# A two-layer hybrid attention trunk: o^T of a chunk loaded and split earlier, a layer's first scores held back longer

## The chip, the cores and the metric

The kernel runs on one core of a Trainium2 chip. Its engines are TensorE (PE: matmuls and transposes; PEld is the loading of its weights), VectorE (DVE), ScalarE (ACT), GpSimd (POOL) and SyncE (SP), which here only issues DMAs. Each engine works through its own queue in order and waits on semaphores for the others. The metric is the device time of one execution in microseconds (us), the median of several runs.

## The reference

Sixteen learned tokens are put ahead of a sequence of 1024, so there are 1040 positions of width 1024, in float32. Then come two layers and a last norm:

```python
for l in range(DEPTH):                       # 2 layers
    hn = rmsnorm(h, norm_gain[l])
    proj = hn @ w_in[l]
    dq, dk, dv, dg, fq, fk, fv, ff, fg = jnp.split(proj, split_points, axis=-1)
    # group 1: 4 differential heads, two softmaxes each, rotary on 16 of 64 columns
    do = diff_attention(rope(dq), rope(dk), dv, lam, chunk_ids)   # p0 - lam * p1
    do = rmsnorm(do, subln_gain[l]) * (1.0 - lam_init) * silu(dg)
    # group 2: 8 forgetting heads, causal, bias from a running sum of log-sigmoids
    fo = forgetting_attention(fq, fk, fv, cumsum(log_sigmoid(ff + b)), positions) * silu(fg)
    h = h + jnp.concatenate([do, fo], axis=-1) @ w_out[l]
out = rmsnorm(h, final_gain)[:, N_META:N_META + seq]
```

## The kernel before

Everything is kept transposed, features on the partitions and positions along the free axis. The 1040 positions are three chunks, c = 0, 1, 2, of 336, 384 and 320 columns, and nine blocks of at most 128. A float32 product is made of three passes over parts rounded to fewer bits: a tensor is split into `hi` (a rounded copy, by ACT) and `lo` (what is left, by a subtraction on DVE or POOL), and hi x hi, lo x hi and hi x lo are summed. So a projection of one chunk for 128 output features is 8 x 3 = 24 matmuls (`mtile`), and gives the processor back after every 6. The split activations of chunk c lie in the tiles `acth` and `actl`, one pair of buffers for each chunk.

A layer has eight head pairs p: 0 to 3 are the differential heads, 4 to 7 two forgetting heads each. For each pair there are projections k, q and a gate g, and four v units of two pairs each. In `q_unit` and `k_unit` a differential head's chunk is turned by `rotate`: ACT copies it out of PSUM, DVE shuffles, POOL and DVE multiply, DVE adds, and then ACT and DVE split it. `Unit` is one attention step (pair, head, chunk): scores on PE, the smallest entry found and the bias added on DVE (tile `mn`), the exponential on ACT, the turn of the probabilities on PE (`transp`, tile `tp`), their split by ACT and DVE (`ath`, `atl`), and the product with v on PE (`av`, tile `po`). Three PSUM banks hold scores. `finish` writes o^T of that step to DRAM (`oscr`).

PE's order is written out while the program is built. `attention` yields, before each step, the time at which it could run and what it needs, and `layer` fills in projections from `fills` until the clock of a small model, `pe.t`, has come that far; a ratio spreads the projections over the pairs. `when[...]` says when a result will be there: for q of a chunk it is `pe.t` plus `LROT` or `LFOX`. The other engines' orders come from a list scheduler, which may put an instruction ahead of earlier ones.

When all projections are placed, `fills` goes on to the output projection. `hc_load` brings the residual of a chunk from DRAM, `out_load` four of the eight 128-row pieces of o^T, into the chunk's `actl` tile, and `out_split` splits them; for the first four (the differential heads) it first loads a row of norm factors from `nscr`, broadcast to a tile `tc`, and multiplies. `tc` has three buffers, which gates and rotations use too. Then `out_main` makes 8 x 24 matmuls of the chunk, with weights loaded and split on the way, and `out_tail` makes the next layer's activations, or the output.

The step has three parts here. (1) Chunks 0 and 1 get their `hc_load`, `act_tiles` and first `out_load` one after the other, each followed by 4.52 us of the model's time (`OL`) before its `out_split`. (2) For each chunk, when its last pair is done, the second `out_load` and `out_split` follow. (3) The model waits `OW` = 7.53 us after the chunk's last gate or pair, and `out_main` starts. Of chunk 2, part (1) comes behind `out_main` of chunk 0.

Of the kernel before, what the change touches and what calls it, by code (L numbers as in the profile page):

```python
# [54 lines left out]
LS, LSC, LT, L1S, LROT, LFOX = ((1.9, 0.0033), (3.4, 0.0042)), 0.7, 2.4, 4.87, 8.0, 5.61  # L55
OT1, OT2, OT3, OW, OL = 2.46, 4.57, 2.54, 7.53, 4.52

LLF, LCUM, LHN = 13.0, 10.0, 8.0
CMAX, SLACK, RMIN, RMAX, STEP, FR0, FR1 = 3.17, 0.4, 0.03, 2.52, 2, 2, 2
# [27 lines left out]
def trunk_kernel(ctx, tc, x, meta, norm_gain, w_in, fbias, lq1, lk1, lq2, lk2,  # L87
# [87 lines left out]
    pe = Clock()  # L175
    const = {}
    when = {}
# [280 lines left out]
    def q_unit(l, p, acts, box):  # L458
# [5 lines left out]
        for c in range(3):  # L464
# [16 lines left out]
            box["q", p, c] = (qq, ql)  # L481
            when["q", p, c] = pe.t + (LROT if diff else LFOX)
            yield
# [101 lines left out]
    def gate(l, p, acts, box):  # L585
# [18 lines left out]
        for c in range(3):  # L604
# [21 lines left out]
            if keep:  # L626
                box["kept"] += 1
                box["gs", p, c] = g
            yield

# [405 lines left out]
    def fills(l, acts, box, new):  # L1036

        unit = {"k": k_unit, "q": q_unit, "g": gate, "v": v_unit}
        todo = ORDER.replace("|", "").split()
        other = None  # L1040
        while todo:
            u = todo.pop(0)
# [14 lines left out]
            if other is not None and (not todo or todo[0][0] == "v"):  # L1057
                yield from other
                other = None
        ts, hcs = [], []  # L1060
        for c in range(3):
            hcs.append(hc_tiles())
            hc_load(hcs[c], c)
            ts.append(act_tiles(c))
            out_load(l, c, ts[c], 0)
            t0 = pe.t
            while pe.t < t0 + OL and (7, 2) not in box["done"]:
                yield True
            out_split(l, c, ts[c], 0)
            if c == 1:  # L1070
                break
        tail = iter(())
        for c in range(3):
            while (7, c) not in box["done"]:
                yield True
            out_load(l, c, ts[c], 4)
            out_split(l, c, ts[c], 4)
            t0 = max(box["done"][7, c], box["done"].get(("g", c), 0.0))
            while pe.t < t0 + OW and (7, 2) not in box["done"]:
                yield True  # L1080
            ob = []
            yield from weave(out_main(l, c, hcs[c], ts[c], ob), tail)
            drive(tail)
            tail = out_tail(l, c, hcs[c], ob, new)
            if c == 0:
                hcs.append(hc_tiles())
                hc_load(hcs[2], 2)
                ts.append(act_tiles(2))
                out_load(l, 2, ts[2], 0)
                out_split(l, 2, ts[2], 0)  # L1090
# [122 lines left out]
```

## Time and profile before

| | us |
|---|---|
| median of 3 runs | 1607.82 |
| lowest and highest | 1603.9, 1608.37 |
| the profiled execution | 1611.42 |
| its span, first to last instruction | 1609.4 |
| PE busy | 1492.9 (93% of the span) |
| DVE busy | 1047.0 (65%) |
| ACT busy | 827.1 (51%) |
| POOL busy | 689.3 (43%) |
| mean granted TensorE clock | 0.968 |

Busy times of different engines overlap, so they don't add up to the span. A granted clock of 1.0 is the higher of TensorE's two levels, 2.4 GHz, and 0.5 the lower, 1.2 GHz. The profiled execution is 3.6 us above the median of the runs.

### The profile page before, as it was taken

Reading aid. Unit: us, or ns where it says so; the run is one execution under the profiler, and the core shown is the slowest. Engines: PE = TensorE matmul, PEld = TensorE weight load, DVE = VectorE, ACT = ScalarE, POOL = GpSimd, SP = SyncE. Lnnn points to the kernel's source line nnn. Section 1 sums busy time; section 2 is a strip of 40 time slices with the busy share of each in tenths; the row PEclk is TensorE's granted clock in tenths of the full one; section 3 lists DMA queues with packets and bytes.
Section 4 is the critical chain, followed back from the end, with each engine's and each line's share of the span. In section 5 each row is a group of like instructions: output and inputs, shape, how many; then the busy total and the mean of one; then the engine's idle time right before and its main releaser. Section 6 shows DMA issues by size and latency. Waiting matters only on the chain.

```text
span 1609.4 us, 30140 instructions
## 1 busy us (share of the span) xinstructions
PE 1492.9 (93%) x9932; PEld 1421.5 (88%) x9932; DVE 1047.0 (65%) x3026; ACT 827.1 (51%) x2067; POOL 689.3 (43%) x1125
## 2 busy tenths in 40 slices
PE   5988999899999999897898999998999999997997
PEld 4888999898999999887888899998899999996897
DVE  6488867765746565767565986685656555657564
ACT  6455555544655565543334655554455545654543
POOL 3353422313444344456755353230344442443664
PEclk9999999999999999989999999999999999997999
DMA  9242311312232323555434232130322332334554
GB/s 241 65 112 68 100 46 44 63 32 81 63 69 67 100 59 99 154 177 145 142 80 95 73 82 80 35 78 20 69 65 70 55 94 57 92 115 141 154 151 138
DMA packets 181180, 147.72 MB, mean 92 GB/s; under 512 B 19592, under 2 KB 176576, under 8 KB 181024
## 3 DMA queue, kind: packets, MB, share of 16 engines
q1 hardware_dynamic: 180416, 143.60, 33.8%
q10 hardware_dynamic: 608, 2.20, 0.4%
q8 instruction: 79, 1.29, 0.3%
q14 instruction: 77, 0.63, 0.1%
HBM read 117.36 MB, written 28.38 MB: 91 GB/s over the span
## 4 chain that ended last, share of the span: by engine, by line
PE 33%; DVE 10%; DMA 6%; issue 4%; POOL 3%; ACT 2%; SPq 0%; ACTq 0%; DVEq 0%; POOLq 0%
PE pj L181 22%; PE po L181 4%; PE sc L181 4%; PE tp L185 3%; DMA wst<-in_w_out_dram 2%; DVE wlo L265 1%; DVE e L656 1%; POOL wlo L265 1%; DMA oscr<-ta 1%; DMA wst<-in_w_in_dram 1%; DVE kt L430 1%; DMA tc<-nscr 1%; DVE actl L430 1%; DMA cb<-in_rope_dram 1%; DVE atl L748 1%
## 5 line engine op out<-in xcount | busy, mean ns | idle before, releaser
L181 PE MATMUL pj<-acth,whi 128*128 128x320 f32 (+2 forms) x1536 | 518.8, 338 | 14.7 <-DVE hc L943 9.3
L181 PE MATMUL pj<-acth,wlo 128*128 128x320 f32 (+2 forms) x1536 | 498.3, 324 | 0.4 <-DVE wlo L265 0.3
L181 PE MATMUL pj<-actl,whi 128*128 128x320 f32 (+2 forms) x1536 | 497.8, 324 | 0.0
L265 POOL TENSOR_TENSOR wlo<-wst,whi 128x256 fp32r<-128x256 f32 (+1 forms) x320 | 250.8, 792 | 242.2 <-ACT whi L261 155.3
L181 PEld LDWEIGHTS pj<-acth,whi 128*128 128x128 f32 x1536 | 296.0, 193 | 18.3 <-DVE hc L943 6.5
L181 PEld LDWEIGHTS pj<-acth,wlo 128*128 128x128 f32 x1536 | 295.6, 192 | 1.8 <-POOL wlo L265 0.7
L181 PEld LDWEIGHTS pj<-actl,whi 128*128 128x128 f32 x1536 | 294.2, 192 | 0.0
L664 ACT ACTIVATE e<-e,mn 80x80 f32<-80x80 f32 (+8 forms) x288 | 225.2, 782 | 133.9 <-DVE mn L656 131.6
L748 DVE TENSOR_TENSOR atl<-tp,ath 128x320 fp32r<-128x320 f32 (+8 forms) x432 | 190.6, 449 | 98.5 <-ACT ath L747 94.8
L747 ACT ACTIVATE ath<-tp 128x320 fp32r<-128x320 f32 (+8 forms) x432 | 166.9, 403 | 150.2 <-PE tp L185 143.1
L261 ACT ACTIVATE whi<-wst 128x256 fp32r<-128x256 f32 (+1 forms) x304 | 124.7, 414 | 133.6 <-DMA wst<-in_w_out_dram 54.1
L181 PE MATMUL sc<-kt,qq 128*128 128x296 f32 (+9 forms) x480 | 176.0, 369 | 18.2 <-DVE mn L656 11.9
L185 PE MATMUL tp<-ident,e 128*128 128x128 f32 (+2 forms) x1080 | 182.0, 276 | 6.1 <-DVE e L716 4.6
L697 POOL TENSOR_SCALAR e<-e,rl 80x80 f32<-80x80 f32 (+2 forms) x144 | 109.1, 758 | 166.8 <-DVE rl L696 165.7
L181 PE MATMUL po<-ath,v 128*128 128x256 f32 (+5 forms) x576 | 166.7, 330 | 13.2 <-ACT ath L747 13.0
L181 PE MATMUL pj<-whi,acth 128*128 128x256 f32 (+3 forms) x576 | 168.0, 292 | 5.4 <-DVE v L430 4.2
L181 PE MATMUL pj<-wlo,acth 128*128 128x256 f32 (+3 forms) x576 | 165.6, 288 | 2.0 <-POOL wlo L265 1.0
L181 PE MATMUL pj<-whi,actl 128*128 128x256 f32 (+3 forms) x576 | 165.4, 287 | 1.8 <-POOL actl L406 0.9
L181 PE MATMUL po<-atl,v 128*128 128x256 f32 (+5 forms) x432 | 138.5, 321 | 22.4 <-DVE atl L748 22.1
L181 PE MATMUL sc<-kt,ql 128*128 128x296 f32 (+9 forms) x480 | 158.1, 331 | 0.0
L185 PEld LDWEIGHTS tp<-ident,e 128*128 128x128 f32 (+2 forms) x1080 | 137.5, 140 | 12.6 <-DVE e L716 5.4
L265 DVE TENSOR_TENSOR wlo<-wst,whi 128x256 fp32r<-128x256 f32 (+1 forms) x128 | 87.7, 691 | 60.0 <-POOL whi L263 53.9
(167 smaller groups left out, 2479.9 us busy)
## 6 DMA issues: line engine op xcount, KB each, us to landing
wst<-in_w_in_dram SPq DMA_DIRECT2D x256, 128.0 KB
wst<-in_w_out_dram SPq DMA_DIRECT2D x192, 128.0 KB
cb<-in_rope_dram SPq DMA_DIRECT2D x20, 320.0 KB
cb<-cscr SPq DMA_DIRECT2D x12, 520.0 KB
cb<-in_rope_dram SPq DMA_DIRECT2D x16, 384.0 KB
oscr<-ta SPq DMA_DIRECT2D x26, 160.0 KB
cb<-in_rope_dram SPq DMA_DIRECT2D x12, 336.0 KB
oscr<-ta SPq DMA_DIRECT2D x20, 192.0 KB
```

The source lines that it names most:

```text
L181: nc.tensor.matmul(o, a, b, start=start, stop=stop)
L185: nc.tensor.transpose(o, a, idn)
L261: nc.scalar.activation(hi, sg_, AF.Copy)
L265: eng.tensor_tensor(lo, sg_, hi.bitcast(F32), ALU.subtract)
L430: nc.vector.tensor_tensor(lo, src, hi.bitcast(F32), ALU.subtract)
L656: nc.vector.tensor_tensor_reduce(e[rows, a:b], pt[rows, :b - a], bias(a, b)[rows, :], op0=ALU.add, op1=ALU.min, scale=1.0, scalar=least, a ...
L664: nc.scalar.activation(e[rows, :ext], e[rows, :ext], AF.Exp, scale=-1.0, bias=mn[rows, len(pcs) - 1:len(pcs)], accum_out=l[rows, :])
L697: nc.gpsimd.tensor_scalar(e[rows, :ext], e[rows, :ext], r[rows, 0:1], 1.0, ALU.mult, ALU.mult)
L747: nc.scalar.activation(ah[:kz, n0:w], tp[:kz, n0:w], AF.Copy)
L748: nc.vector.tensor_tensor(al[:kz, n0:w], tp[:kz, n0:w], ah[:kz, n0:w].bitcast(F32), ALU.subtract)
```

## The change

A new function `early(c)` is called by `gate`, when the last of the eight gates of a chunk is placed, for chunks 0 and 1. It does the chunk's `hc_load`, `act_tiles`, and both parts of `out_load` and `out_split`; the second part only if the chunk's last pair is done by then. The wait `OL` is gone. What could not be loaded then is loaded inside the loop over `out_main`'s steps of an earlier chunk, as soon as the last pair of that chunk is done, or at the old place. Besides, the first pair's q counts as ready 6.0 us later in the model (`LQ0`), so that PE's order holds more projections ahead of a layer's first scores.

```diff
--- before.py
+++ after.py
@@ -53,9 +53,9 @@
 
 
 LS, LSC, LT, L1S, LROT, LFOX = ((1.9, 0.0033), (3.4, 0.0042)), 0.7, 2.4, 4.87, 8.0, 5.61
-OT1, OT2, OT3, OW, OL = 2.46, 4.57, 2.54, 7.53, 4.52
-
-LLF, LCUM, LHN = 13.0, 10.0, 8.0
+OT1, OT2, OT3, OW = 2.46, 4.57, 2.54, 7.53
+
+LLF, LCUM, LHN, LQ0 = 13.0, 10.0, 8.0, 6.0
 CMAX, SLACK, RMIN, RMAX, STEP, FR0, FR1 = 3.17, 0.4, 0.03, 2.52, 2, 2, 2
 COST = {"k": 11.4, "q": 11.4, "g": 11.4, "v": 25.7, "h": 0.0}
 FADD = [0.0, 0.0, 0.0, 0.0, 0.0, 0.0, 0.0, 20.0]
@@ -479,7 +479,7 @@
                 nc.gpsimd.tensor_scalar(qq[s][ro, o:w], qq[s][r, o:w].bitcast(F32), 1.0, 1.0,
                                         ALU.mult, ALU.mult)
             box["q", p, c] = (qq, ql)
-            when["q", p, c] = pe.t + (LROT if diff else LFOX)
+            when["q", p, c] = pe.t + (LROT if diff else LFOX) + LQ0 * (p == 0)
             yield
 
 
@@ -626,6 +626,9 @@
             if keep:
                 box["kept"] += 1
                 box["gs", p, c] = g
+            box["gd"][c] += 1
+            if box["gd"][c] == 8 and c < 2:
+                box["early"](c)
             yield
 
 
@@ -1038,6 +1041,20 @@
         unit = {"k": k_unit, "q": q_unit, "g": gate, "v": v_unit}
         todo = ORDER.replace("|", "").split()
         other = None
+        ts, hcs, whole = [], [], set()
+
+        def early(c):
+
+            hcs.append(hc_tiles())
+            hc_load(hcs[c], c)
+            ts.append(act_tiles(c))
+            for k0 in (0, 4):
+                if k0 == 0 or (7, c) in box["done"]:
+                    out_load(l, c, ts[c], k0)
+                    out_split(l, c, ts[c], k0)
+                    if k0:
+                        whole.add(c)
+        box["gd"], box["early"] = [0] * 3, early
         while todo:
             u = todo.pop(0)
             now = head_norms(l, box) if u == "h" else unit[u[0]](l, int(u[1]), acts, box)
@@ -1057,29 +1074,25 @@
             if other is not None and (not todo or todo[0][0] == "v"):
                 yield from other
                 other = None
-        ts, hcs = [], []
-        for c in range(3):
-            hcs.append(hc_tiles())
-            hc_load(hcs[c], c)
-            ts.append(act_tiles(c))
-            out_load(l, c, ts[c], 0)
-            t0 = pe.t
-            while pe.t < t0 + OL and (7, 2) not in box["done"]:
-                yield True
-            out_split(l, c, ts[c], 0)
-            if c == 1:
-                break
         tail = iter(())
         for c in range(3):
             while (7, c) not in box["done"]:
                 yield True
-            out_load(l, c, ts[c], 4)
-            out_split(l, c, ts[c], 4)
+            if c not in whole:
+                whole.add(c)
+                out_load(l, c, ts[c], 4)
+                out_split(l, c, ts[c], 4)
             t0 = max(box["done"][7, c], box["done"].get(("g", c), 0.0))
             while pe.t < t0 + OW and (7, 2) not in box["done"]:
                 yield True
             ob = []
-            yield from weave(out_main(l, c, hcs[c], ts[c], ob), tail)
+            for _ in weave(out_main(l, c, hcs[c], ts[c], ob), tail):
+                for i in range(len(ts)):
+                    if i not in whole and (7, i) in box["done"]:
+                        whole.add(i)
+                        out_load(l, i, ts[i], 4)
+                        out_split(l, i, ts[i], 4)
+                yield
             drive(tail)
             tail = out_tail(l, c, hcs[c], ob, new)
             if c == 0:
```

At the end of layer 0, PE's queue in the second last attention unit (pair 7, chunk 2, first head). `po` is the product with v, `tp` the turned probabilities; an output projection of chunk 0 reads `acth`/`actl` with `whi`/`wlo`. Before:

```order
L181 MATMUL sc<-cb_67 128x128
L181 MATMUL po<-ath,v 128x320
L181 MATMUL po<-atl,v 128x320
L185 MATMUL tp<-ident,e 128x128 x3
L181 MATMUL po<-ath,v 128x320
L181 MATMUL po<-atl,v 128x320
L185 MATMUL tp<-ident,e 128x128 x3
```

The same place in the changed kernel:

```order
L181 MATMUL po<-atl,v 128x320
L185 MATMUL tp<-ident,e 128x128 x3
L181 MATMUL pj<-acth_8987,whi 128x336
L181 MATMUL pj<-acth_8987,wlo 128x336
L181 MATMUL pj<-actl_8988,whi 128x336
L181 MATMUL pj<-acth_8987,whi 128x336
L181 MATMUL pj<-acth_8987,wlo 128x336
L181 MATMUL pj<-actl_8988,whi 128x336
L181 MATMUL po<-ath,v 128x320
L181 MATMUL po<-atl,v 128x320
```

Before, no projection follows in this unit, and the output projection of chunk 0 begins with the last unit; now 48 of its 192 matmuls stand ahead of the last unit. In layer 1, 30 stood ahead of the last unit, all in the unit before it; now there are 78, and the first 18 stand still another unit earlier. The run of projection matmuls behind the last unit has shrunk from 114 to 84 in layer 0, from 90 to 54 in layer 1.

DVE's queue at the end of layer 0, where the first four pieces of o^T of chunk 0 are scaled (`tc<-actl`) and split (`actl<-tc,acth`). Before, between scores (`e,mn`) and turned probabilities (`atl`) of chunk 2, 320 columns wide:

```order
L656 ISA e,mn<-sc,cb,mn 128x344
L656 ISA mn 128x1
L927 TENSOR_TENSOR tc<-actl_9199,tc 128x336
L656 ISA e,mn<-sc,cb 128x488
L656 ISA mn 128x1
L748 TENSOR_TENSOR atl<-tp,ath 128x320
L927 TENSOR_TENSOR tc<-actl_9199,tc 128x336
```

In the changed kernel, between those of chunk 1, 384 columns wide:

```order
L659 ISA e,mn<-sc,cb,mn 128x344
L659 ISA mn 128x1
L930 TENSOR_TENSOR tc<-actl_8988,tc 128x336
L751 TENSOR_TENSOR atl<-tp,ath 128x384
L930 TENSOR_TENSOR tc<-actl_8988,tc 128x336
L659 ISA e,mn<-sc,cb 128x488
L659 ISA mn 128x1
L699 RECIPROCAL rl<-ls 128x1
L930 TENSOR_TENSOR tc<-actl_8988,tc 128x336
L430 TENSOR_TENSOR actl_8988<-tc,acth_8987 128x336
```

They have moved one attention unit forward, and the first of them now stands ahead of an `atl`.

DVE's queue at layer 0's first scores. `ql_87` and `ql_88` are splits of q of chunk 1, `ql_89` and `ql_90` of chunk 2; shapes of 336 columns behind them belong to k of pair 1, chunk 0. Before:

```order
L423 TENSOR_TENSOR tc<-tc 128x384
L430 TENSOR_TENSOR ql_87<-tc,qq 64x384
L656 ISA e,mn<-sc,dm_69 80x80
L656 ISA mn 80x1
L656 ISA e,mn<-sc,dm_69 80x80
L656 ISA mn 80x1
```

In the changed kernel:

```order
L430 TENSOR_TENSOR ql_88<-tc,qq 64x384
L420 STREAM_SHUFFLE tc<-tc 128x320
L422 TENSOR_TENSOR tc<-tc,cb 128x320
L423 TENSOR_TENSOR tc<-tc 128x320
L420 STREAM_SHUFFLE tc<-tc 128x336
L430 TENSOR_TENSOR ql_89<-tc,qq 64x320
L422 TENSOR_TENSOR tc<-tc,cb 128x336
L430 TENSOR_TENSOR ql_90<-tc,qq 64x320
L423 TENSOR_TENSOR tc<-tc 128x336
L659 ISA e,mn<-sc,dm_69 80x80
L659 ISA mn 80x1
```

The rotation of q of chunk 2 and that of k of pair 1, chunk 0, have come to stand ahead of the first scores' evictions. On PE 42 projection matmuls (24 of 336 columns and 18 of 384) have moved ahead of the first scores, in both layers.

## Rows read from the trace of the kernel before

**Rows 1.** TensorE's waits over the whole run: us in total, times, longest.

```profile
PE po L181 <- DVE atl L748: 22.1, 21, 3.1
...
PE sc L181 <- DVE mn L656: 11.9, 13, 3.8
```

**Rows 2.** Windows: length, busy PE PEld DVE ACT POOL; PE clock, DMA share, GB/s.

```profile
660.00:680.00 20.00, 18.85 (x119) 16.92 (x117) 15.19 (x47) 11.76 (x28) 9.66 (x13) 1.00 0.63 194
680.00:698.00 18.00, 12.46 (x51) 10.39 (x50) 14.27 (x35) 9.86 (x24) 4.75 (x9) 0.62 0.64 193
712.24:726.30 14.06, 14.06 (x92) 13.78 (x90) 5.70 (x9) 4.45 (x12) 8.82 (x13) 1.00 0.84 254
712.30:822.40 110.10, 93.16 (x539) 89.53 (x538) 69.60 (x129) 39.25 (x94) 79.91 (x110) 0.93 0.54 156
1456.00:1490.00 34.00, 21.65 (x103) 17.88 (x101) 26.20 (x62) 16.69 (x40) 12.20 (x19) 0.75 0.41 122
1507.12:1520.46 13.34, 13.34 (x92) 13.08 (x90) 6.42 (x11) 6.46 (x15) 8.68 (x13) 1.00 0.79 230
100.00:140.00 40.00, 36.09 (x218) 32.88 (x218) 37.36 (x107) 24.18 (x55) 12.21 (x17) 1.00 0.29 71
```

**Rows 3.** Windows of five stretches at the lower clock.

```profile
683.80:697.40 13.60, 10.40 (x39) 8.77 (x38) 11.45 (x28) 7.45 (x18) 4.58 (x8) 0.50 0.60 188
1458.60:1465.40 6.80, 4.67 (x18) 4.59 (x19) 2.83 (x6) 1.41 (x5) 3.93 (x7) 0.50 0.20 55
1475.70:1485.90 10.20, 5.74 (x19) 4.94 (x20) 7.82 (x15) 5.84 (x13) 2.91 (x5) 0.50 0.28 72
93.30:100.10 6.80, 4.63 (x17) 4.63 (x18) 5.72 (x23) 4.71 (x15) 5.33 (x8) 0.50 0.84 109
878.30:885.20 6.90, 5.31 (x19) 5.31 (x20) 5.51 (x25) 5.33 (x17) 5.07 (x11) 0.51 0.59 118
```

**Rows 4.** Windows at both layer ends, instructions on tile actl alone.

```profile
655.00:700.00 45.00, 10.27 (x30) 6.20 (x30) 12.79 (x24) 3.37 (x8) 0.00 (x0) 0.85 0.58 178
1450.00:1490.00 40.00, 6.88 (x18) 4.52 (x18) 14.20 (x24) 3.47 (x8) 0.00 (x0) 0.79 0.48 142
```

**Rows 5.** Groups of DVE by shape, 655 to 700: busy us, mean ns, idle before.

```profile
L430 DVE TENSOR_TENSOR actl<-tc,acth 128x336 fp32r<-128x336 f32 x4 | 3.2, 808 | 0.0
L927 DVE TENSOR_TENSOR tc<-actl,tc 128x384 f32<-128x384 f32 x4 | 2.2, 553 | 2.1 <-DMA tc<-nscr 2.1
...
L430 DVE TENSOR_TENSOR actl<-actl,acth 128x336 fp32r<-128x336 f32 x4 | 1.8, 504 | 1.3 <-ACT acth L428 1.3
```

**Rows 6.** Timeline of DVE at 1457.6: start, us, what.

```profile
1457.64 2.57 DVE L265 TENSOR_TENSOR wlo<-wst,whi 128x256 fp32r<-128x256 f32 x1
```

**Rows 7.** Timeline of POOL around 1458.

```profile
1457.13 1.00 POOL L623 TENSOR_TENSOR ta<-ta,gs 64x384 f32<-64x384 f32 x1 [1.68 <-DVE gs L619]
...
1459.21 0.72 POOL L265 TENSOR_TENSOR wlo<-wst,whi 128x256 fp32r<-128x256 f32 x1
```

**Rows 8.** Chain of waits, layer 1's end: start, us, what.

```profile
1448.95 4.69 DMA actl<-oscr
```

**Rows 9.** Chain of waits, layer 0's end.

```profile
678.05 3.91 DMA tc<-nscr
```

**Rows 10.** Timeline of PE, layer 0's fourth score; idle before it in brackets.

```profile
95.47 0.58 PE L181 MATMUL sc<-kt,qq 128*128 128x256 f32 x1 [3.77 <-DVE mn L656]
```

**Rows 11.** Timeline of PE, layer 1's first and fourth scores.

```profile
874.75 0.35 PE L181 MATMUL sc<-kt,qq 128*80 128x256 f32 x1 [1.05 <-POOL qq L479]
...
879.89 0.58 PE L181 MATMUL sc<-kt,qq 128*128 128x256 f32 x1 [3.78 <-DVE mn L656]
```

**Rows 12.** Timeline of DVE ahead of layer 0's first eviction.

```profile
92.72 1.06 DVE L423 TENSOR_TENSOR tc<-tc 128x384 f32<-128x384 f32 x1 [0.88 <-POOL tc L421]
...
95.17 0.24 DVE L656 CUSTOM_DVE_ANT_0 e<-sc,dm 80x80 f32<-80x80 f32 x1
```

**Rows 13.** Timeline of POOL, product for q of chunk 2.

```profile
97.76 1.12 POOL L421 TENSOR_TENSOR tc<-tc,cb 128x320 f32<-128x320 f32 x1
```

## The prediction

> **What bounds the kernel now.** I read the engines' totals first, then TensorE's waits, then windows by stage, then the timeline at the places found. PE is busy for 1492.9 of 1609.4 us, so about 116 us of idle time, and what the lower clock takes after it, are all that an order of work can win. The largest wait is a product with v that waits for DVE's split of the turned probabilities; scores that wait for an eviction by DVE are the next that bear on the change [rows 1]. The windows show where they lie. At the end of layer 0, PE is busy for 12.46 of 18.00 us at a clock of 0.62; at the end of layer 1, for 21.65 of 34.00 us at 0.75, while the stretch from 100 to 140 has 36.09 of 40.00 [rows 2]. In the two layer ends PE has attention to do and nothing to fill in: the gates are done and the output projection has not begun.
>
> The loss there, at full clock, is the idle time plus half of what was busy at the lower clock. Layer 0: 18.00 - 12.46 = 5.5 idle, and 10.40 / 2 = 5.2 [rows 2, 3], together 10.7 us. Layer 1: 34.00 - 21.65 = 12.4, and (4.67 + 5.74) / 2 = 5.2, together 17.6 us. These are ceilings for the first part of the change.
>
> **Output projection moved forward.** In layer 0, 48 matmuls of 336 columns now stand ahead of the last attention unit where none did. Ninety such matmuls without a wait took 14.06 us [rows 2], so one is 0.156 and the 48 are 7.5 us. The work is not new; it fills a gap and leaves the tail behind. If the unit takes as long as before, the gain is 7.5 us; bounds are 0 and 10.7. I take 7.5. In layer 1, 78 stand there instead of 30; the 48 more, at 13.34 / 90 = 0.148 [rows 2], are 7.1 us. But here more is lost than that, and most of DVE's splits of o^T leave the stretch too, which shortens its own waits. Between 7.1 and the ceiling of 17.6 I take 10, near the lower end. Sum of both: -17.5, bounds 0 and -28.3.
>
> What is late next is DVE. Loading and splitting o^T of chunks 0 and 1 is the same 24 DVE instructions in a layer as before, 12.79 us in layer 0 and 14.20 in layer 1 [rows 4], and they go forward into units in which DVE already has 15.19 of 20 us [rows 2]. It can be filled further: from 100 to 140 it was busy for 37.36 of 40. But behind each such instruction wait evictions and `atl` splits, and PE for these. They add nothing where a gate's projection still covers them, and at most their whole duration: 0 to 12.8 and 0 to 14.2. The nearest rows are one instruction's length, about 0.5 to 0.8 [rows 5], and the wait of the scaling for its factor row, 2.1 us over four of them [rows 5]. I take 3 us for each layer, +6. The DMAs are the same in number; the loads of the factor rows now go out on SP right behind the first load of o^T, ahead of some weight loads. Those are hidden as long as four of them are ahead of PE.
>
> A place in the trace shows what could make this larger. At 1457.64 a subtraction on DVE with two inputs in SBUF took 2.57 us; three instructions ran on POOL from 1457.13 to 1459.93 [rows 6, 7]. The 24 moved ones are of that sort, and four of them took 808 ns where four others took 504 [rows 5]. The Trainium skill ("SBUF — State Buffer", section "Who interferes with whom") says that a DVE instruction with two SBUF inputs contends with a GpSimd instruction that reads SBUF, and that one of the two waits for the other's whole length. The trace agrees in the 2.57 us. By that rule the 24 get longer where POOL is busier. What that would make of the time is the first rival.
>
> **First scores held back.** Before, PE's fourth score waits 3.77 us in layer 0 and 3.78 in layer 1, where the first waits 1.05 more [rows 10, 11]; five us of these stretches are busy at the lower clock [rows 3]. The names say that two more projections should cover this. The order says otherwise: they bring their rotation with them, and DVE does q of chunk 2 and most of k of pair 1, chunk 0, ahead of the first eviction. I follow DVE through its new order; its shuffles, products, sums and splits of a chunk take about half a us each. The two splits of q of chunk 1 end at about 96.0, as before without the two evictions between. Shuffle and product of chunk 2 take it to 97.1; its sum waits for POOL's product, which stands behind two weight splits in either order and ends at 97.76 + 1.12 = 98.9 [rows 13], and ends at 99.4. The next shuffle, two splits and a product come to 101.5; the last sum waits for POOL, which has a copy of q and a product to do after ACT's split at 99.9 and is ready at about 102.1. The first eviction then ends at about 102.8 instead of 95.4 [rows 12]. PE has used 42 matmuls more by then: 24 x 0.156, and 18 at 384 / 336 x 0.156, 7.0 us. So the fourth score is 7.4 us later for 7.0 us of work done earlier: +0.4 in layer 0. Layer 1, done in the same way from its own times, gives the same; I put +0.8 for both. On the way PE now also waits for a PSUM bank ahead of the second new projection, because ACT's copy stands behind splits that wait for DVE; that lies inside the 7.4. Ceiling of the gain: waits and lower clock gone, 3.77 + 4.63 / 2 = 6.1 and 1.05 + 3.78 + 5.31 / 2 = 7.5 [rows 3, 10, 11], -13.6. Floor: one more chunk of rotation in the way, which the first eviction's delay behind the last sum bounds at 95.17 - 92.72 = 2.5 [rows 12], for each layer +5.
>
> The projections done early are missing later: between the first turned probabilities of pair 0 and those of pair 1, 24 fewer stand in PE's order, 3.7 us. There DVE is the fuller engine (37.36 of 40 against 36.09 [rows 2]), so PE may wait as much longer; but the rotations are gone from DVE as well. Between 0 and 3.7 I take 1 for each layer, +2.
>
> **Sum.** -17.5 + 6 + 0.8 + 2 = -8.7 us. The profiled execution took 1611.42, its span 1609.4; so it would be 1602.7. The median of the runs is 3.6 below the profiled one, and the forecast is 1607.8 - 8.7 = 1599. Its own range is 1593 to 1604.
>
> **Rivals.** First: DVE takes back what PE wins. If each of the 24 moved instructions is longer by 808 - 504 = 0.3 us [rows 5], that is 7.3 us a layer instead of 3: -17.5 + 14.6 + 0.8 + 2 = -0.1, 1608. For it speaks that POOL is busy for 9.66 of 20 us in the stretch that the splits move into and 4.75 of 18 in that which they leave [rows 2]; against it, that gates still cover part of that stretch. The out projection gives the same time in another way, if it is bound by its weights: from 712.3 to 822.4 PE is idle for 16.9 us [rows 2], and starting earlier would only lengthen that.
>
> Second, slower: the transfers hold DVE. The scaling stands ahead of an `atl` now, and needs o^T, 4.69 us from issue, and its factor row, 3.91 beside it [rows 8, 9]. If DVE comes to it when these have just gone out, every `atl` and eviction behind it is late by 4.69 for each of the two chunks, 9.4 a layer; a lower clock after it cost 4.67 / 2 = 2.3 at 1458.6 [rows 3]; with the 3 us above that is 14.7 a layer: -17.5 + 29.4 + 2.8 = +14.7, 1622. The sum turns positive once a chunk's wait passes 2.2 us: (17.5 - 2.8 - 6) / 4. Against it: between the last gate of a chunk and that place PE has some 4 us of matmuls, so that most of the transfer is over.
>
> Third: the first scores' wait goes, as the edit's name has it. Then -13.6 stands for +0.8, and the sum is -23.1: 1585. Against it speaks DVE's order alone.
>
> **How the numbers follow.** The forecast has a chance of 0.50, the first rival 0.22, the second 0.15, the third 0.13. 0.3% of the time, about what a measurement of this kernel can tell from no change, is 4.8 us: 1603.0 and 1612.6. Of the forecast 0.46 lies below that, all 0.13 of the third rival, and 0.02 of the first: faster 0.61. The second's 0.15 and 0.02 of the first are slower: 0.17. The rest, 0.22, is no change. From 1584 to 1613 leaves out most of the second rival and the lower half of the third, 0.2.
>
> **What would show it.** Right: at the end of layer 0 PE runs at full clock or near it through the second last unit, with 6 or 12 output projections between its products, and the run behind the last unit is 84 matmuls long; in layer 1, 54. DVE's scalings of chunk 0 stand some 13 us earlier, with under 2 us of idle time ahead of the first. At the first scores PE still waits 3 to 4 us for tile `mn`, and DVE's first eviction ends 7 us later than before. The forecast is wrong if DVE waits for `nscr` or `oscr` by more than 3 us at a time in the units of pair 7, if PE's waits for `atl` in chunk 1's units grow by more than 3 us a layer, or if the wait for `mn` is gone.

## The result, and the profile after

The changed kernel takes 1593.89 us (median of 6 runs, 1591.37 to 1599.08), the kernel before on the same chip 1608.09 (6 runs, 1603.9 to 1610.42). The ratio is 0.9917 with a 95% interval of 0.9896 to 0.9938: 14.2 us won, where 8.7 were forecast. The profiled execution took 1591.37 us, its span is 1589.6.

Windows of five stretches: first the start, where no instruction of TensorE's order has changed, then the end of layer 0 (from pair 7, chunk 1, second head, to the row sums behind chunk 0's output), pair 1 and pair 3 of layer 1, and the end of layer 1 (from pair 7, chunk 1, first head, to the last product with v). Columns as in [rows 2]. Before:

```profile
0.00:71.14 71.14, 51.68 (x331) 44.27 (x331) 40.71 (x122) 39.07 (x98) 25.94 (x40) 0.95 0.63 166
661.85:738.57 76.72, 65.90 (x393) 61.46 (x392) 49.61 (x114) 35.55 (x85) 40.18 (x64) 0.91 0.60 182
958.42:1032.02 73.60, 70.45 (x496) 69.36 (x496) 47.92 (x151) 36.55 (x97) 21.52 (x37) 0.98 0.26 70
1101.21:1186.60 85.39, 81.68 (x574) 78.91 (x574) 48.87 (x170) 37.82 (x99) 22.31 (x44) 0.98 0.23 51
1439.51:1506.88 67.37, 54.95 (x332) 50.09 (x331) 47.51 (x118) 35.21 (x84) 27.73 (x47) 0.87 0.45 133
```

The changed kernel, same stages:

```profile
0.00:68.74 68.74, 51.91 (x330) 45.00 (x331) 41.22 (x122) 38.82 (x98) 24.65 (x40) 1.00 0.65 172
658.11:732.13 74.02, 65.34 (x401) 61.48 (x399) 48.36 (x114) 35.84 (x86) 39.73 (x62) 0.93 0.64 191
959.58:1028.24 68.66, 66.90 (x468) 65.73 (x466) 49.25 (x150) 36.70 (x95) 22.27 (x39) 1.00 0.25 69
1101.98:1178.39 76.41, 75.18 (x550) 72.99 (x548) 49.79 (x172) 36.21 (x96) 18.73 (x39) 1.00 0.22 46
1428.56:1493.58 65.02, 57.40 (x356) 53.43 (x355) 47.40 (x123) 38.77 (x90) 33.79 (x55) 0.92 0.47 140
```

Length less PE's busy time is idle time; half of what is busy at the lower clock is lost besides. Worked out so from the records of PE and of its clock, every stage has a loss in us. This table has it for all kernels of the study, which the next section describes; each row is one execution, and the stages together are the whole span. "Pairs" reaches from a layer's first product with v to the layer's end, "out" from there on (in layer 0 to the row sums of chunk 1, after which the stage of layer 1's first scores begins).

| kernel | start | first scores L0 | pairs L0 | end L0 | out L0 | first scores L1 | pairs L1 | end L1 | out L1 | sum |
|---|---|---|---|---|---|---|---|---|---|---|
| before | 22.7 | 6.3 | 21.4 | 16.0 | 12.5 | 17.4 | 25.9 | 17.7 | 15.5 | 155.5 |
| changed | 16.8 | 6.3 | 21.2 | 12.5 | 13.6 | 16.0 | 19.6 | 12.7 | 15.2 | 134.1 |
| lq0_only | 19.8 | 7.2 | 25.0 | 16.0 | 12.6 | 14.5 | 21.5 | 15.7 | 15.2 | 147.5 |
| early_only | 17.1 | 5.2 | 21.2 | 11.5 | 11.9 | 18.8 | 23.8 | 9.7 | 16.8 | 136.0 |
| no_fill | 22.5 | 7.3 | 22.2 | 19.1 | 12.0 | 17.7 | 21.0 | 14.5 | 17.3 | 153.6 |
| split_late | 23.0 | 6.2 | 22.0 | 18.6 | 16.4 | 18.5 | 19.1 | 20.2 | 17.1 | 161.2 |
| no_rot | 19.3 | 1.5 | 20.5 | 11.1 | 16.2 | 12.4 | 19.3 | 10.0 | 16.5 | 126.7 |
| rows_hi | 18.9 | 7.5 | 21.8 | 12.6 | 10.4 | 15.6 | 20.0 | 12.1 | 14.1 | 133.1 |
| lq12_only | 21.3 | 5.2 | 12.9 | 19.3 | 11.8 | 16.5 | 14.4 | 16.1 | 18.0 | 135.7 |
| lq0_12 | 21.4 | 5.3 | 12.9 | 10.6 | 11.6 | 15.6 | 14.4 | 11.2 | 14.8 | 117.7 |
| lq0_18 | 20.7 | 3.9 | 16.8 | 12.6 | 11.6 | 15.4 | 13.2 | 12.8 | 16.6 | 123.6 |
| rows_lq12 | 21.4 | 5.5 | 14.8 | 16.1 | 8.9 | 19.1 | 14.1 | 11.2 | 14.9 | 126.0 |
| early_cb_sp | 22.6 | 5.7 | 20.5 | 10.7 | 11.4 | 16.7 | 18.9 | 9.7 | 16.9 | 133.1 |
| lq12_cb_sp | 18.8 | 5.4 | 13.0 | 10.3 | 14.0 | 15.6 | 14.9 | 9.2 | 16.8 | 118.1 |

The start varies from 16.8 to 23.0 us among kernels that do the same there, so the 5.9 us between the first two rows are chance of one execution. The end of layer 0, too, lost 16.0 to 19.3 us in the three kernels without early loads, 10.3 to 12.6 in eight with both these and the matmuls moved forward, and 16.1 in a ninth (rows_lq12): two rows that differ by 3 us in one stage prove little alone. Without the start the traces differ by 15.5 us, and the medians by 14.2. Of the 15.5, 8.5 are at the two layer ends, and 6.3 in the pairs of layer 1, where the forecast had nothing.

PE's waits after, as in [rows 1]:

```profile
PE po L181 <- DVE atl L751: 15.1, 15, 2.6
...
PE sc L181 <- DVE mn L659: 9.4, 7, 3.6
```

The first has fallen from 22.1 us. That total does not measure the layer ends: it is 15.1 us in lq0_only and 14.7 in early_only, which have one part of the change each. The second kept its longest, and the fourth score of each layer shows where (PE's timeline, as in [rows 10, 11]):

```profile
100.51 0.39 PE L181 MATMUL sc<-kt,qq 128*128 128x256 f32 x1 [3.63 <-DVE mn L659]
...
881.52 0.39 PE L181 MATMUL sc<-kt,qq 128*128 128x256 f32 x1 [3.63 <-DVE mn L659]
```

DVE's timeline ahead of layer 0's first eviction, as in [rows 12]:

```profile
96.28 0.49 DVE L423 TENSOR_TENSOR tc<-tc 128x320 f32<-128x320 f32 x1 [1.47 <-POOL tc L421]
...
99.67 0.51 DVE L423 TENSOR_TENSOR tc<-tc 128x336 f32<-128x336 f32 x1 [0.78 <-POOL tc L421]
100.21 0.24 DVE L659 CUSTOM_DVE_ANT_0 e<-sc,dm 80x80 f32<-80x80 f32 x1
```

Both last sums of the two rotations wait for POOL's products, and the eviction follows at once, as the prediction had it.

At the end of layer 0, DVE's instructions on tile actl from 645 to 705: duration in ns (least, median, most), first and last start. Before:

```profile
L927 DVE TENSOR_TENSOR tc<-actl,tc x8: 494/527/559, 682.1 to 697.4; 128x336 f32<-128x336 f32 x4, 128x384 f32<-128x384 f32 x4
L430 DVE TENSOR_TENSOR actl<-tc,acth x8: 488/548/1203, 684.6 to 698.7; 128x336 fp32r<-128x336 f32 x4, 128x384 fp32r<-128x384 f32 x4
...
  DMA tc<-nscr: 3.7, 3
```

After:

```profile
L930 DVE TENSOR_TENSOR tc<-actl,tc x8: 493/526/559, 663.4 to 685.5; 128x336 f32<-128x336 f32 x4, 128x384 f32<-128x384 f32 x4
L430 DVE TENSOR_TENSOR actl<-tc,acth x8: 496/548/1312, 665.8 to 688.3; 128x336 fp32r<-128x336 f32 x4, 128x384 fp32r<-128x384 f32 x4
...
  DMA tc<-nscr: 5.1, 2
```

The scalings begin 18.7 us earlier, 3.7 of which the trace was already ahead (661.85 and 658.11 in the windows), so 15 where 13 were forecast; and none takes longer (527 and 526 ns in the median). The last line of each says what DVE stood for ahead of them: 3.7 us in three waits for a factor row before, the longest 1.8, and 5.1 us in two after. The longer of these two (DVE's timeline):

```profile
685.53 0.56 DVE L930 TENSOR_TENSOR tc<-actl,tc 128x384 f32<-128x384 f32 x1 [3.23 <-DMA tc<-nscr]
```

All 24 scalings and splits of a layer took DVE 12.79 and 14.20 us before [rows 4], and 13.15 and 15.52 after (windows, instructions on tile actl alone):

```profile
650.00:700.00 50.00, 13.75 (x42) 8.42 (x42) 13.15 (x24) 3.36 (x8) 0.00 (x0) 0.90 0.60 180
1425.00:1485.00 60.00, 17.75 (x53) 10.90 (x52) 15.52 (x24) 3.36 (x8) 0.00 (x0) 0.91 0.49 146
```

PE pays for the early splits one unit earlier than it used to lose its time. From chunk 1's first product with v in layer 0's pair 7 to chunk 2's it lost 1.1 us before and 6.8 after; from there to the last unit's first product 10.8 before and 4.3 after, and the granted clock in that stretch rose from 0.69 to 0.92. The waits after (PE's timeline of layer 0's units of chunk 1 and 2):

```profile
672.32 0.55 PE L181 MATMUL po<-ath,v 128*128 128x256 f32 x1 [2.66 <-ACT ath L750]
...
674.40 0.55 PE L181 MATMUL po<-atl,v 128*128 128x256 f32 x1 [1.53 <-DVE atl L751]
...
688.42 0.64 PE L181 MATMUL po<-atl,v 128*128 128x320 f32 x1 [2.56 <-DVE atl L751]
```

The first of these waits goes back to ACT, which stood for the second load of o^T with `ath` queued behind it (ACT's timeline):

```profile
670.03 0.48 ACT L428 ACTIVATE acth<-actl 128x336 fp32r<-128x336 f32 x1 [1.85 <-DMA actl<-oscr]
```

### The profile page after: what moved, and what is told of

It reads as the page before. It is cut to its first block, busy times and chain, and to the rows that moved or that the text cites. A ratio compares the mean times of both kernels' runs of the same rounds, so it can differ in the third digit from the quotient of the medians.

```text
span 1589.6 us, 30114 instructions
## 1 busy us (share of the span) xinstructions
PE 1484.5 (93%) x9932; PEld 1417.3 (89%) x9932; DVE 1044.9 (66%) x3026; ACT 828.5 (52%) x2067; POOL 688.1 (43%) x1125
## 4 chain that ended last, share of the span: by engine, by line
PE 60%; DVE 14%; DMA 9%; issue 8%; POOL 5%; ACT 2%; SPq 1%; DVEq 0%; POOLq 0%; ACTq 0%
PE pj L181 38%; PE sc L181 8%; PE po L181 7%; PE tp L185 6%; DMA wst<-in_w_in_dram 3%; POOL wlo L265 2%; DMA tc<-nscr 2%; DVE e L659 2%; DMA oscr<-ta 1%; POOL tc L421 1%; DMA actl<-oscr 1%; DVE wlo L265 1%; DVE e L663 1%; DVE e L719 1%; DVE kt L430 1%
## 5 line engine op out<-in xcount | busy, mean ns | idle before, releaser
L181 PE MATMUL pj<-acth,whi 128*128 128x320 f32 (+2 forms) x1536 | 516.9, 336 | 17.1 <-DVE hc L946 10.1
L181 PEld LDWEIGHTS pj<-acth,whi 128*128 128x128 f32 x1536 | 295.1, 192 | 21.4 <-DVE hc L946 9.1
L181 PE MATMUL sc<-kt,qq 128*128 128x296 f32 (+9 forms) x480 | 177.0, 372 | 14.8 <-DVE mn L659 9.4
L181 PE MATMUL po<-ath,v 128*128 128x256 f32 (+5 forms) x576 | 164.8, 327 | 11.5 <-ACT ath L750 11.2
L181 PE MATMUL po<-atl,v 128*128 128x256 f32 (+5 forms) x432 | 136.6, 316 | 17.3 <-DVE atl L751 15.1
```

Of the source, the lines that this page charges most:

```text
L181: nc.tensor.matmul(o, a, b, start=start, stop=stop)
```

## The experiments

All are compared with the kernel before on the chip that they ran on. A ratio of 0.001 is 1.6 us.

**lq0_only**: the third edit without the first two.

```diff
 (kernel before)
+LQ0 = 6.0
-            when["q", p, c] = pe.t + (LROT if diff else LFOX)
+            when["q", p, c] = pe.t + (LROT if diff else LFOX) + LQ0 * (p == 0)
```

> The kernel before with the 6.0 us of LQ0 added to when the first pair's q counts as ready, and nothing else; the loads and splits of o^T stay where they were. Theory of the prediction: +0.8 for the first scores and +2 for the thinner fill in pair 0, +2.8 us, a ratio of 1.002 (0.999 to 1.004); PE still waits 3 to 4 us for mn at the fourth score of each layer. Rival A, from the two traces (pair 0 to pair 4 of both layers gave back some 8 us in the changed kernel, which the layer ends cannot have done): LQ0 is worth -5 to -8 us, a ratio of 0.995 to 0.997, and the gain shows between the first products of pair 1 and pair 4. Rival B: what the pairs gave is noise of one execution, and the ratio is within 0.002 of 1.

Measured: 1605.35 us, ratio 0.9981 (0.9968 to 0.9995), so -3.1 us, and not +2.8. The wait for `mn` stayed (longest 3.9 us). What rival A said of the size was too much, of the place half right: the pairs of layer 1 lose 21.5 us instead of 25.9, but those of layer 0 lose 25.0 instead of 21.4. Rival B's band holds the ratio as well, and the interval barely leaves out 1; but what the pairs do is no noise of one execution. From one pair's first product to the next one's, pair 6 of layer 0 lost 0.7 to 0.8 us in the three kernels with LQ0 = 0 and 4.0 to 4.7 in all six with LQ0 = 6; layer 1's pair 1 lost 3.6 to 4.8 and 1.7 to 1.8.

**early_only**: the first two edits without the third.

```diff
 (changed kernel)
-LLF, LCUM, LHN, LQ0 = 13.0, 10.0, 8.0, 6.0
+LLF, LCUM, LHN, LQ0 = 13.0, 10.0, 8.0, 0.0
```

> The changed kernel with LQ0 = 0: o^T is loaded and split early, the first scores stand where they stood before. Theory of the prediction: -17.5 + 6 = -11.5 us, a ratio of 0.993 (0.989 to 0.996). Rival A (LQ0 carries half of the gain): -6 to -8 us, a ratio of 0.995 to 0.996. Rival B (all of it is the layer ends): -14 us, 0.991, as the changed kernel. If the two parts add, this run's change and that of LQ0 alone give -14.2 us together.

Measured: 1596.28 us, ratio 0.9916 (0.9895 to 0.9937), -13.5 us. This agrees with the prediction's -11.5 and with rival B; the two layer ends lose 21.2 us instead of 33.7, by 12.5 less. So the early loads alone give as much as the whole change. The two parts do not add up to it (-3.1 - 13.5 = -16.6 against -14.2), but the intervals are too wide to make anything of 2.4 us. By the same ratios LQ0 = 6 added nothing to the early loads (0.9917 and 0.9916).

**no_fill**: o^T early, the output projections not.

```diff
 (changed kernel)
+            while c == 0 and (7, 2, 0) not in box["fin"]:
+                yield True
             ob = []
             for _ in weave(out_main(l, c, hcs[c], ts[c], ob), tail):
```

> The changed kernel, but out_main of chunk 0 may not start before the second last attention unit (pair 7, chunk 2, first head) is finished, so that no output projection stands ahead of the last unit; loads and splits of o^T stay early. It separates what the moved matmuls give from what the early splits cost. Theory of the prediction: the gain of 17.5 us goes and the cost of the early splits stays, so 1593.9 + 17.5 = 1611 us, a ratio to the kernel before of 1.002 (1.000 to 1.005), somewhat more as layer 1's 30 matmuls ahead of the last unit go as well. Rival A (from the two traces: the layer ends gave 6 to 8.6 us net): 1600 to 1603, a ratio of 0.995 to 0.997. Rival B: the gain at the layer ends came from splits that no longer stand among the last units' work on DVE, not from PE's fill: 1595 to 1598, 0.992 to 0.994.

Measured: 1610.21 us, ratio 1.0006 (0.9989 to 1.0022). The theory holds and both rivals fall: what the matmuls that stand ahead of the last unit give is (1.0006 - 0.9917) x 1608 = 14.3 us, where the prediction had 17.5 for the moved ones alone; the 14.3 include the 30 that stood there before. The traces put 6.6 of it at layer 0's end and 1.8 at layer 1's; the rest is spread and not assigned. Against lq0_only, which differs by the early splits and by layer 1's 30 matmuls, the time is (1.0006 - 0.9981) x 1608 = 4.0 us longer. Layer 0's end loses 19.1 us instead of 16.0, but lq12_only, without early splits, loses 19.3 there. In chunk 1's units of layer 0 alone it is 6.2 us instead of 3.4 (1.1 in the kernel before), so that a cost of about 3 us a layer fits the runs but is not measured closely.

**split_late**: the output projections early, the splits not.

```diff
 (changed kernel, in early)
                     out_load(l, c, ts[c], k0)
-                    out_split(l, c, ts[c], k0)
+                    held.append((c, k0))
...
+        for c, k0 in held:                  # behind the loop over todo
+            out_split(l, c, ts[c], k0)
         tail = iter(())
```

> The changed kernel, with o^T of chunks 0 and 1 loaded at the last gate as there, but split (and scaled) only when all gates are placed, so that on DVE the scalings of layer 0's chunk 0 stand some 28 instructions later, in the units of chunk 2 as before. TensorE's order is the same to the instruction, so the output projections of chunk 0 still stand ahead of the last unit. Theory: the early splits are what lets these matmuls run; without them PE waits for them in the second last unit of layer 0, and the +3 us a layer that they cost in chunk 1's units come back at most: slower than the changed kernel by 3 to 8 us, 0.994 to 0.997. Rival: most of what the early splits cost is DVE waiting for transfers that have just gone out; later splits find them landed, and the time is that of the changed kernel or up to 4 us less, 0.989 to 0.992.

Measured: 1612.77 us, ratio 1.0018 (1.0 to 1.0036), so 16 us more than the changed kernel, twice the most that the theory had, and the rival is out. PE's timeline shows the price at the first output projection of each layer:

```profile
689.44 0.65 PE L181 MATMUL pj<-acth,whi 128*128 128x336 f32 x1 [6.23 <-ACT acth L428]
...
1469.13 0.64 PE L181 MATMUL pj<-acth,whi 128*128 128x320 f32 x1 [5.45 <-ACT acth L428]
```

Here PE, in order, stands for the split itself, and all of attention behind it stands too; the two ends lose 38.8 us instead of 25.2. The splits and the fill are one edit; each alone leaves the time where it was, and 4 and 6 us above lq0_only, which has the third edit as they have.

**no_rot**: what holds the first eviction. This kernel leaves out the turn of two chunks, so its output is another.

```diff
 (changed kernel, in rotate; turn is False for q of pair 0, chunk 2, and k of pair 1, chunk 0)
         nc.scalar.activation(v, pt[:, o:o + w], AF.Copy, scale=scale)
+        if not turn:
+            return t
         t2 = st("tc", CW)
```

> The changed kernel without the turn (shuffle, two products, sum) of q of pair 0, chunk 2, and of k of pair 1, chunk 0, in both layers; these two chunks are only copied and split, so the output is another. TensorE's order is the same to the instruction. It takes away what the prediction says keeps the wait at the first scores. Theory of the prediction: DVE's first eviction ends some 4 us earlier, the wait for mn falls from 3.6 us to under 1 in both layers, and with the low clock behind it the time falls by 7 to 10 us against the changed kernel, 1584 to 1587 (0.985 to 0.987). Rival: the wait comes from the chain of evictions and the exponential itself; it stays above 2.5 us and the time is within 3 us of the changed kernel, 0.990 to 0.993.

Measured: 1583.74 us, ratio 0.9834 (0.9813 to 0.9854), 13 us under the changed kernel, where 7 to 10 were expected. The fourth score in both layers:

```profile
98.01 0.39 PE L181 MATMUL sc<-kt,qq 128*128 128x256 f32 x1
...
877.42 0.39 PE L181 MATMUL sc<-kt,qq 128*128 128x256 f32 x1
```

No wait stands in brackets any more. The stages of the first scores lose 13.9 us instead of 22.3. At LQ0 = 6 it is the rotations that DVE does first which keep this wait, and the rival falls; these stages give 8.4 us of the trace, and the rest of the 13 lies in the others and is not assigned.

**lq0_12** and **lq0_18**: more of the third edit; **lq12_only**: without the early loads.

```diff
 (changed kernel; lq12_only: kernel before with the same line)
-LLF, LCUM, LHN, LQ0 = 13.0, 10.0, 8.0, 6.0
+LLF, LCUM, LHN, LQ0 = 13.0, 10.0, 8.0, 12.0          # lq0_18: 18.0
```

> The changed kernel with LQ0 = 12.0 for 6.0, which puts 36 more projection matmuls (5.6 us) ahead of the first scores of each layer. Theory of the prediction: they bring their rotations, which DVE does first, and the wait for mn at the fourth score stays at 3 to 4 us; the time is that of the changed kernel within 3 us, 1592 to 1597 (0.990 to 0.993). Rival A: with cover enough the wait goes and the clock stays up, -6 us or more against the changed kernel, 1588 (0.987). Rival B: the fill is used up for pairs 0 and 1, +5 us, 1599 (0.994).

> The changed kernel with LQ0 = 18.0. Theory A (cover): what LQ0 gives is the wait at the first scores, 3.6 us a layer at 6 and about 2.4 at 12; at 18 it is under 1 us, and the time falls by 3 us or more against LQ0 = 12, to 1577 (0.981) or below. Theory B (phase): LQ0 moves the whole later fill against the attention, and waits of 1 to 3 us between pair 1 and pair 4 come and go with it; then there is no trend, and the time lies between 1580 and 1596 (0.983 to 0.992), with the difference to LQ0 = 12 in the stages of pairs 1 to 7 and not at the first scores. Theory C: the fill is used up and pair 0 starves, above 1596.

> The kernel before with LQ0 = 12.0 alone, without the early loads of o^T. It tells whether the two parts add. Theory: they add; early loads gave 0.0064 to 0.0084 of the time at LQ0 = 6 and 0, so this is 0.9828 + 0.0075 = 0.990 (0.988 to 0.993), 1592 us, and the gain lies at the first scores of both layers and in pairs 0 to 4. Rival A: LQ0 alone stays worth 3 us whatever its size, 0.998, and the two parts help each other. Rival B: the earlier loads give nothing at LQ0 = 12, 0.983.

Measured: lq0_12 1580.92 us, ratio 0.9828 (0.9805 to 0.9852); lq0_18 1583.1 us, 0.983 (0.9811 to 0.985); lq12_only 1589.96 us, 0.9873 (0.9859 to 0.9888). The theory that put lq0_12 level with the changed kernel is wrong by 14 us; rival A allows the size (6 us or more), but not the place. Its fourth scores:

```profile
112.00 0.39 PE L181 MATMUL sc<-kt,qq 128*128 128x256 f32 x1 [2.35 <-DVE mn L659]
...
877.44 0.58 PE L181 MATMUL sc<-kt,qq 128*128 128x256 f32 x1 [0.89 <-DVE mn L659]
```

The wait is shorter, but the first scores as a stage gave only 1.4 us (5.3 + 15.6 against 6.3 + 16.0). The pairs gave 13.5 (27.3 against 40.8), and lq12_only, rows_lq12 and lq12_cb_sp repeat it with 27.3 to 28.9. At 18 the wait is gone in both layers, with all rotations in place, and the time did not fall further: the first scores lose 19.3 us, 3.0 less than at 6, and layer 0's pairs lose more than at 12, 16.8. That is theory B, phase: where a projection falls against the attention beside it counts, and not only how much stands ahead. Single pairs show it, since their losses do not follow the amount. From LQ0 = 0 to 6, 12 and 18, pair 6 of layer 0 lost 0.8, 4.5, 0.4 and 0.4 us (the first from early_only), and layer 1's pair 0 5.1, 7.6, 4.1 and 2.0; kernels with the same LQ0 agree within 0.7 us in the one and, but for no_rot, within 0.4 in the other. What pair 6 has at 6 alone is this (PE's timeline of the changed kernel):

```profile
591.76 0.38 PE L181 MATMUL po<-ath,v 128*128 128x256 f32 x1 [2.71 <-ACT ath L750]
```

At 12 the early loads gave (0.9873 - 0.9828) x 1608 = 7.2 us, against 10.3 found at 6 (0.9981 - 0.9917) and 13.5 at 0. The intervals overlap, so the runs neither refute that the two parts add nor exclude a gain that falls as LQ0 grows; lq12_only itself lies just under its expected range.

**early_cb_sp** and **lq12_cb_sp**: one of the waits that come and go with the phase. With LQ0 = 0, PE waits ahead of layer 1's pair 4 for ath. Timeline of ACT in the kernel before; the second row is ACT's queue issuing a load:

```profile
1157.07 0.79 ACT L747 ACTIVATE ath<-tp 80x320 fp32r<-80x320 f32 x2 [0.90 <-PE tp L185]
1162.51 1.09 ACTq L824 DMA_DIRECT2D cb<-cscr  x2
1163.64 0.43 ACT L428 ACTIVATE qq<-pj 64x320 fp32r<-64x320 f32 x1 [5.79 <-issue]
1164.62 0.43 ACT L428 ACTIVATE qq<-pj 64x320 fp32r<-64x320 f32 x1 [0.55 <-DVE ql L432]
1165.08 0.77 ACT L747 ACTIVATE ath<-tp 128x320 fp32r<-128x320 f32 x2
```

That the load stands for a store shows with the early loads alone, where the same row names it:

```profile
1155.68 0.43 ACT L428 ACTIVATE qq<-pj 64x320 fp32r<-64x320 f32 x1 [6.00 <-DMA cscr<-cb]
```

PE's waits for that and, in pair 1, for a gate's eviction; before:

```profile
970.81 0.69 PE L181 MATMUL pj<-acth,whi 128*128 128x384 f32 x1 [2.58 <-DVE tc L619]
...
1165.57 0.63 PE L181 MATMUL po<-ath,v 128*128 128x320 f32 x1 [3.09 <-ACT ath L747]
```

and with the early loads alone:

```profile
965.24 0.45 PE L181 MATMUL pj<-acth,whi 128*128 128x384 f32 x1 [3.00 <-DVE tc L619]
...
1157.61 0.42 PE L181 MATMUL po<-ath,v 128*128 128x320 f32 x1 [3.30 <-ACT ath L750]
```

Neither stands in the traces of the changed kernel, lq0_only or lq0_12. The load is moved to another queue:

```diff
 (early_only; lq12_cb_sp: lq0_12)
-                        load = nc.scalar.dma_start if u.p == 4 else dma
+                        load = dma
```

> The early loads with LQ0 = 0, and the loads of the first two bias rows of pair 4 (cb<-cscr) issued on SP instead of ACT. TensorE's order is the same to the instruction. In the traces with LQ0 = 0, ACT stands 6 us ahead of this load until the store of cscr has landed, with the split ath behind it, and PE waits 3.1 to 3.3 us for ath ahead of layer 1's pair 4; in those with LQ0 = 6 or 12 ACT waits 0.4 to 0.9 us there. Theory (this is one of the waits that LQ0 removed by shifting the fill): PE's wait for ath there goes, and with the low clock behind it the time falls by 3 to 5 us against the early loads alone, 0.9916 to 0.9885 to 0.990. Rival: SP now stands for the store, with weight loads behind it, and PE waits for weights instead: the time stays at 0.991 to 0.993 or rises.

> The same edit in the changed kernel with LQ0 = 12.0, where ACT waits 2.1 us in layer 0 and 0.9 us in layer 1 at this place and PE has no wait for ath from it. Theory: nothing to win, the ratio stays at 0.983 within 0.002. Rival: ACT's place matters beyond the one wait: 0.980 or below.

Measured: early_cb_sp 1591.26 us, ratio 0.9896 (0.9876 to 0.9916), 3 us less than early_only; the intervals overlap, but the trace is clear. All that PE waits for from layer 1's first product of pair 3 to that of pair 4:

```profile
PE sc L181 <- DVE e L663: 0.9, 2, 0.7
```

The wait of 3.3 us for ath is gone, and that stretch loses 1.0 us instead of 6.0. SP's queue now stands 4.6 us for the store and PE does not notice. lq12_cb_sp took 1577.86 us, 0.9825 (0.9804 to 0.9846), as its theory had it: where the phase has already removed the wait, there is nothing to win.

**rows_hi** and **rows_lq12**: the factor rows out of DVE's way.

```diff
 (changed kernel; rows_lq12: lq0_12)
+            for k in range(4):                              # in out_load, if k0 == 0
+                dma(out=t[0].bitcast(F32)[:, k, :],
+                    in_=nscr[l, k:k + 1, CS[c]:CE[c]].to_broadcast([P, w]))
...
-                dma(out=t2[:, :w], in_=nscr[l, k:k + 1, CS[c]:CE[c]].to_broadcast([P, w]))
-                nc.vector.tensor_tensor(t2[:, :w], of[:, k, :], t2[:, :w], ALU.mult)
+                nc.vector.tensor_tensor(t2[:, :w], of[:, k, :], hi.bitcast(F32)[:, k, :], ALU.mult)
```

> The changed kernel, but the four factor rows are loaded into the chunk's acth tile, which is free then and is overwritten by the split behind, and not into tc, of which there are three buffers for gates and rotations too; so all four go out with the load of o^T. TensorE's order is the same to the instruction. Theory (from the trace of the changed kernel: at layer 0's end DVE waits 1.89 and 3.23 us for tc<-nscr, and PE behind it loses 11 us from the first head of chunk 1 to the last unit): DVE waits under 1 us for a factor row, and the time falls by 2 to 5 us against the changed kernel, 1589 to 1592 (0.988 to 0.990). Rival: what holds there is ACT, whose split waits 1.85 us for the second load of o^T with ath queued behind it; the time is the same within 1.5 us, 0.991 to 0.993.

> The changed kernel with the two edits that made it faster, together: LQ0 = 12.0 and the four factor rows loaded into the chunk's acth tile with the load of o^T. If they add, 0.9828 - (0.9917 - 0.9870) = 0.978, 1573 us (0.975 to 0.981). Rival: rows in acth gave only what the other rerun of DVE's order gave by chance (in its trace the stall at layer 0's end had not shrunk), and the ratio is that of LQ0 = 12, 0.981 to 0.985.

Measured: rows_hi 1589.09 us, 0.987 (0.9851 to 0.9888); rows_lq12 1580.51 us, 0.9835 (0.9814 to 0.9857). The first time is what the theory asked for, but the trace denies its mechanism. DVE's waits at layer 0's end in rows_hi:

```profile
DVE tc L933 <- DMA actl<-oscr: 2.7, 1, 2.7
...
DVE tc L933 <- DMA acth<-nscr: 1.5, 1, 1.5
```

4.2 us instead of 5.1: with the rows out of the way DVE stands for o^T itself. The end of layer 0 loses 12.6 us, as before the edit (12.5); the only stage that lost clearly less is the output of layer 0, 10.4 instead of 13.6, and there the other kernels lie anywhere from 8.9 to 16.4. With LQ0 = 12 the edit gave nothing, as its rival said. The interval of rows_hi lies under the changed kernel's, but what made it faster stays open.

The fastest versions, apart from no_rot, which leaves work out, are lq12_cb_sp, lq0_12, lq0_18 and rows_lq12. They cannot be told apart: 0.9825 to 0.9835, some 27 us under the kernel before.

## Why the prediction was right, and where not

The time was 1593.9 for a forecast of 1599.0, within the range and at the lower end of its own, 1593 to 1604. Its main mechanism is shown; one small term had the wrong place and sign. The early part, forecast at -11.5, gave -13.5 alone and -10.3 with LQ0 = 6; the third edit, forecast at +2.8, gave -3.1 alone and nothing clear on top of the early loads.

**Output projection forward, -17.5.** Shown by no_fill: 14.3 us, layer 1's older 30 matmuls included. As forecast the gain needs the early splits (split_late). At the end of layer 0 the 48 matmuls gave 6.6 us (19.1 in no_fill, 12.5) for 7.5 forecast. The 10 of layer 1 is not borne out as fill: its end lost 12.7 us instead of 14.5 in no_fill. What fell there is the second last unit, 11.4 us before (7.3 in lq0_only), 5.3 in no_fill and 4.1 after, so that in these traces more of it came with the splits leaving that unit, the prediction's other reason, than with the fill.

**DVE's splits earlier, +3 a layer.** By the times the early splits of both layers and the loss of layer 1's older 30 matmuls cost 4.0 us together (no_fill against lq0_only, give or take 3.4 by the two intervals), where 6 were forecast for the splits. In layer 0 the cost came more as waits for transfers than as longer instructions: DVE's waits for factor rows grew from 3.7 to 5.1 us, and ACT stood 1.85 us for a load of o^T with ath behind it. So the second rival's mechanism is there, at a third of the 9.4 us a layer that it was given. One of the signs against the forecast was met: a single wait of 3.23 us for a factor row is just over the 3 us named. PE's waits for `atl` in chunk 1's units grew by 1.7 us in each layer, under the 3 named for them. At layer 1's end no cost is seen (14.5 us in no_fill, 15.7 in lq0_only).

**First scores, +0.8.** The stages lost 0.0 us more in layer 0 and 1.4 less in layer 1. DVE's order kept the wait, 3.63 us against the 3.77 and 3.78 before, for the reason given: the fourth score came 5.0 us later in layer 0 (95.47 and 100.51), and no_rot shows that it is the two rotations. The first eviction ended at 100.45 and not at 102.8, but the start had already run 2.4 us faster (71.14 and 68.74 for the same work); with these 2.4 us the eviction is at the forecast 102.8, and the score comes the forecast 7.4 us later. That more cover brings its own rotations holds at 6 only: at 18 the wait is gone.

**Thinner fill, +2: the step that failed.** The prediction looked for the price of 24 projections missing in pair 0, and nowhere else. There it was near: pair 0 lost 2.2 us less in layer 0 and 2.5 more in layer 1. But later projections move too, and pairs far down the layer gain or lose waits with them. In layer 1 this removed the 2.58 us wait in pair 1 and the 3.09 us wait in pair 3 with the low clock behind them; pairs 1 and 3 lost 1.8 and 1.2 us after, 4.7 and 5.2 before. Pair 6 of layer 0 lost 3.8 us more. Instead of +2.8, this term and the first scores' +0.8 together, LQ0 alone gave -3.1 us, and at 12 it gave -20.4 (0.9873). The trace of before shows both waits, and names what they wait for; what it could not show is that they would go. With the early loads the losses of both layers' pairs went 45.0, 40.8, 27.3, 30.0 us in all from 0 to 6 to 12 to 18, so a bound of 0 to 3.7 a layer was far too narrow.

**Rivals.** The first (DVE takes it back) is out at its size: the 24 instructions took 0.4 us more in layer 0 and 1.3 more in layer 1, not 7.3 (in the median 526 and 548 ns in layer 0, 527 and 548 before), and the output of layer 0 lost 1.1 us more, not the whole gain. The third (the first scores' wait goes) did not happen; no_rot, where it does, is 13 us faster, but only 8.4 of that lies in the two stages for which 13.6 was worked out as a ceiling.

## What to carry to other kernels

Work that fills a gap of the bottleneck needs its inputs made ready earlier too; either edit without the other gave nothing or a loss, so test them as one. When an order is planned by a running credit, holding back one step shifts all that follows: list every wait of 2 us or more downstream of the edit, not just the place edited, and try several sizes, since what comes and goes there can be larger than what the edit is for. A load that must wait for a store does not belong in the queue of an engine whose next instruction is needed, unless the store is known to have landed.

## What the runs showed of the hardware

The first 70 us, with the same instructions in the same order on PE, lost between 16.8 and 23.0 us in fourteen executions, and the granted clock there lay between 0.93 and 1.00 (0.95 in the one of before, 1.00 in that of the changed kernel). A single trace's difference in this stage is no evidence on a change. A stretch in the middle can repeat far better: pair 6 of layer 0 lost 4.0 to 4.7 us in the six executions with LQ0 = 6 and 0.4 to 0.5 in the four with LQ0 = 12.
